# Output projection of a Hymba-style block as seven 2x2-block products of 512 columns, its weight sums made by GpSimd in an earlier stage

## The chip, the cores and the metric

The kernel runs on one core of one Trainium2 chip. Times are device microseconds (us) of one launch. The kernel before took 1847.0 us, the median of three runs (1839.05 to 1862.62 us). A profiled execution of the same kernel took 1841.22 us; all traces below are of that execution, and its span, from the first to the last instruction, is 1839.4 us. PE is TensorE, DVE is VectorE, ACT is ScalarE, POOL is GpSimd, SP is SyncE, which issues nearly all DMAs. PE, DVE, ACT, POOL and SP each run their own instructions in the order in which the program holds them.

## What is computed

One layer on 1024 frames (T) of width 1024, all in float32: a half-step gated feed-forward (SwiGLU), a mixer with one input projection and one output projection, a second half-step feed-forward, and a final norm.

```python
x = x + 0.5 * swiglu(rmsnorm(x, ffn1_norm[l]), ffn1_w_gate[l], ffn1_w_up[l], ffn1_w_down[l])
h = rmsnorm(x, mix_norm[l])
p = h @ w_in[l]
...
x = x + jnp.concatenate([y_a, y_b], axis=-1) @ w_out[l]
x = x + 0.5 * swiglu(rmsnorm(x, ffn2_norm[l]), ffn2_w_gate[l], ffn2_w_up[l], ffn2_w_down[l])
return rmsnorm(x, final_norm)
```

`y_a` (spatial gating) and `y_b` (gated delta rule) are 512 columns each. The change concerns the line with `w_out`: a product of 1024x1024 by 1024x1024.

## The kernel before

Every float32 product is made as three products of a cheaper type: `split` (L60) turns a tile into a high part (a rounding, ACT, L61) and a low part (source less high part, DVE, L62), and `mm3` (L55) adds high x high, high x low and low x high into one PSUM bank. So each new operand costs ACT and DVE one instruction each before PE can use it.

The program runs in five stretches: the gate/up products of the first feed-forward, its down product, the mixer (`middle`), the output projection, and the second feed-forward with its own gate/up and down products. Both feed-forwards are made of 2x2 blocks with seven products in place of eight (the Strassen-Winograd scheme). For their gate/up part the class `Combos` holds the activation's blocks B11, B12, B21, B22 and the sums T1 to T4: `blocks` (L127) transposes a pair of 128-frame tiles with PE, copies and splits the blocks and forms the sums from PSUM on DVE; `put_sums` (L153) splits the sums, with DVE or GpSimd for the low part. `load_gu` (L181) does the same for the weights: GpSimd forms s1 to s4, ACT and DVE split them.

In the down product, `plan` (L359) lists seven products; each is cut into units of two 128-row blocks. `prepare` (L369) loads a unit's two operands, `left` and `right`, over SP, splits them, and runs three units ahead of PE. During products 3 and 4 of this stage GpSimd has next to nothing to do.

The output projection (`w_out`, L571) uses plain blocks. Two groups of four frame tiles, 0,4,1,5 and 2,6,3,7, are transposed and split once (`to_T`, L98). For each group the 1024 output columns are made in four chunks of 256, each of 8 contraction blocks x 4 tiles x 3 products, so the matmuls have 256 columns, and the weights are loaded and split once for each group. The chunk's result is added to the residual tile `xs[t]` by DVE (L593). The first group's tiles are stored, normed in place, transposed and split for the second feed-forward (L609 to L615) after the second group's first two chunks are under way, so the remaining chunks on PE cover that work. Then `start2` makes chunk 0 of the second feed-forward plainly (`gu_plain`): first 256 frames, then the other 256, whose tiles 2, 6, 3, 7 are normed in between. From chunk 1 on PE runs the seven products without pause.

The order on each engine is not written out by hand: a scheduler of the framework arranges the instructions, within what the buffers allow. Buffers come from pools as rings: `graw` has 4 slots (raw weights), `gsp` 7 (split weights), `post` 4, `cmb` 3, PSUM 4 + 4 banks. An allocation waits until the slot's earlier tile has been read for the last time.

Of the kernel before, what the change touches and what calls it, by code (L numbers as in the profile page):

```python
# [30 lines left out]
def block_kernel(ctx: ExitStack, tc, a, out):  # L31
# [75 lines left out]
    class Combos:  # L107
# [19 lines left out]
        def blocks(self, i, pp, xns, uv, b12=None):  # L127
            def tr(j, q):
                return transposed(pp, lambda c: xns[j][:, (q * 4 + c) * P:(q * 4 + c + 1) * P])
# [35 lines left out]
    def ffn(cb, wgu, wd, ps, rp, gp, qp, bp, start, load_xts, emit, before={}, fill=None):  # L165
# [12 lines left out]
        def gtile(dt, name):  # L178
            return gp.tile([P, 2, 512], dt, tag="gsp", name=name, bufs=7)

        def load_gu(c, plain=False):  # L181
            raw = []
            for j in range(2):
                r = rp.tile([P, 1088], F32, tag="graw", name="graw", bufs=4)[:, :D].rearrange("p (s n) -> p s n", s=2)
                nc.sync.dma_start(r, wgu[c][:, j * 1024:(j + 1) * 1024].rearrange("p (s n) -> p s n", s=2))
                raw.append(r)
            a11, a12, a21, a22 = raw[0][:, 0], raw[0][:, 1], raw[1][:, 0], raw[1][:, 1]

            def comb(n, u, v, op):
                f = rp.tile([P, 544], F32, tag="sf", name=n, bufs=4)[:, :512]  # L190
                nc.gpsimd.tensor_tensor(f, u, v, op=op)  # L191
                return f
# [175 lines left out]

        def prepare(l, r, u):  # L369
# [7 lines left out]
            nc.sync.dma_start(left[:, :n], hq[u][:, l, :n])  # L377
# [22 lines left out]
        for k, (_, _, pp, first, last, ev, then) in enumerate(plan):  # L400
# [43 lines left out]
    sp = {n: dr.tile([8, P, 512], F32, tag="sp" + n, name="sp" + n) for n in "zvm"}  # L444
    ba = cp.tile([P, 16, 8], F32, tag="ba", name="ba")[:, :8]
# [13 lines left out]
    with ExitStack() as f1:  # L459
# [83 lines left out]
        ffn(cb, a["f1gu"], a["f1wd"], ps, rp, gp, qp, bp, start1, load_xts, to_mid, {2: [after]}, z0)  # L543
# [14 lines left out]
    with ExitStack() as f2:  # L558
# [10 lines left out]
        xs = load_x(xd, chain(*order))  # L569

        def w_out(i):  # L571
            for ch in range(4):
                ws = []
                for s in range(2):
                    raw = rp.tile([P, 2, 512], F32, tag="graw", name="graw", bufs=4)
                    nc.sync.dma_start(raw, a["wo"][ch][s].rearrange("p (q n) -> p q n", q=2))
                    for q in range(2):
                        w = gp.tile([P, 2, 512], F32R, tag="gsp", name="wo", bufs=7)
                        split(w[:, 0], w[:, 1], raw[:, q])
                        ws.append(w.rearrange("p s (k n) -> p s k n", k=2))  # L580
                yield
                banks = {t: bank(ps[0], "mm")[:, :256] for t in order[i]}
                steps = [(k, t) for k in range(KC // 2) for t in range(4)]
                if (i, ch) == (1, 3):
                    steps.sort(key=lambda s: s[1])
                for q, j in steps:
                    t = order[i][j]
                    for k in (2 * q, 2 * q + 1):
                        w, y = ws[q], yT[i][k // 4][:, :, k % 4, j * P:j * P + P]
                        mm3(banks[t], y[:, 0], y[:, 1], w[:, 0, k % 2], w[:, 1, k % 2], k == 0, k == KC - 1, skip_group_check=True)  # L590
                    if k == KC - 1:
                        xv = xs[t][:, ch * 256:ch * 256 + 256]
                        nc.vector.tensor_tensor(xv, xv, banks[t], op=ALU.add)  # L593
                yield

        cb = Combos(g2, qp, bp)
        pp = (ps[1], "ax")
        together(w_out(0))
        for t in order[0]:
            nc.sync.dma_start(xd[t], xs[t])  # L600

        def b12():
            ts = [gp.tile([P, 2, 512], F32R, tag="gsp", name="B12", bufs=7) for _ in range(2)]
            return [t.rearrange("p s (k n) -> p s k n", k=2) for t in ts]

        second = w_out(1)
        together(second, n=3)
        b = b12()
# [7 lines left out]
        together(second)  # L616
        for t in order[1]:
            nc.sync.dma_start(xd[t], xs[t])

        def start2(f):  # L620
# [11 lines left out]
            V, G = nc.vector, nc.gpsimd  # L632
# [11 lines left out]
        def fin(t, xt):  # L644
            o = gp.tile([P, D], F32, tag="gsp", name="o", bufs=7)
# [17 lines left out]
        ffn(cb, a["f2gu"], a["f2wd"], ps, rp, gp, qp, bp, start2, load_xts, fin, {2: [after]})  # L663
# [14 lines left out]
def middle(tc, nc, a, L):  # L678
# [513 lines left out]
    for h in range(HEADS):  # L1192
# [32 lines left out]
        else:  # L1225
            stage(x, weave(chain(y.values(), y.queries()), islice(u0, 8), (0, 1, 1, 1, 0)), 1.5)
            stage(y, u0, 1)
            u1 = steps("u", 1, ev_u1, part=2)
# [28 lines left out]
def _layout(np, x, ffn1_norm, ffn1_w_gate, ffn1_w_up, ffn1_w_down, mix_norm, w_in, gm_ln_g, gm_ln_b, gm_w_s,  # L1257
# [6 lines left out]
    def tmaj(cols):  # L1264
# [15 lines left out]
        wo=np.stack([tmaj(w_out[0][:, c * 256:c * 256 + 256]) for c in range(4)]),  # L1280
# [26 lines left out]
```

## Time and profile before

| | |
|---|---|
| median of three runs | 1847.0 us |
| the profiled execution | 1841.22 us |
| its span | 1839.4 us |
| mixer's last product ends on PE (about) | 1077.2 us from the span's start |
| output projection ends on PE | 1185.0 us |
| chunk 1 of the second feed-forward starts | 1218.1 us |

The three times in the last rows are read from the timeline of PE. In such a timeline a row gives start, length, engine, line, operation, output, inputs, shapes and count, and in brackets the idle time ahead of it with what ended it. Successive instructions overlap a little, so a row's pace is its length, or the distance to the next start, divided by its count. Where a busy table gives a group's mean duration, that is the latency of one instruction, not its pace.

### The profile page before, as it was taken

To read this page: it belongs to the slowest core of one execution; us is meant where nothing else is said; L and a number is where in the kernel's file an instruction comes from. 1 tells how busy PE (TensorE), PEld (TensorE's weight loads), DVE (VectorE), ACT (ScalarE), POOL (GpSimd) and SP (SyncE) were. 2 spreads that over 40 slices of the span, in tenths; PEclk is the share of its full clock that TensorE was granted. 3 is DMA by queue.
4 is the path that set the end of the run, shared out by engine and by line. 5 is a ranking of instruction groups with operands and counts; after the bars stand their busy time and mean duration, and the time that the engine had idled before them with its cause. 6 is when DMAs were issued, how large, how long until landed. Compare 5 with 4: busy or idle time off the path is not lost.

```text
span 1839.4 us, 25484 instructions
## 1 busy us (share of the span) xinstructions
PE 1784.1 (97%) x9735; PEld 1524.8 (83%) x9735; DVE 1191.7 (65%) x1531; ACT 686.6 (37%) x1193; POOL 747.9 (41%) x583
## 2 busy tenths in 40 slices
PE   5999999999999999898999999999999999999997
PEld 4888888888788889797788989988888888878886
DVE  6867676665565575769655344587776766656546
ACT  6333332333343454432344533452333323243433
POOL 4667666565140012212132420366666665614001
PEclk9999999999999999999999999999999999999999
DMA  5353443544957445453432254334535445495744
GB/s 196 108 175 136 162 152 134 184 158 163 339 188 258 155 177 164 140 195 100 133 94 67 90 197 136 109 104 165 178 132 171 144 154 188 142 344 185 264 142 149
DMA packets 134441, 302.26 MB, mean 164 GB/s; under 512 B 27408, under 2 KB 42032, under 8 KB 134320
## 3 DMA queue, kind: packets, MB, share of 16 engines
q1 hardware_dynamic: 131824, 296.20, 46.9%
q10 hardware_dynamic: 2496, 4.44, 0.8%
q8 instruction: 76, 1.25, 0.3%
q14 instruction: 45, 0.37, 0.1%
HBM read 208.83 MB, written 91.77 MB: 163 GB/s over the span
## 4 chain that ended last, share of the span: by engine, by line
PE 78%; DVE 8%; DMA 5%; POOL 4%; issue 3%; ACT 2%; SPq 0%; POOLq 0%; DVEq 0%; ACTq 0%
PE mm L53 43%; PE ax L53 32%; POOL s L191 1%; POOL t L278 1%; DMA left<-hq 1%; DVE acc L873 1%; PE ax L95 1%; PE sd L53 1%; DMA graw<-in_f1gu_dram 1%; POOL s L278 1%; PE sc L53 1%; DVE T L119 0%; DVE unit L62 0%; DVE wk L62 0%; DVE E L797 0%
## 5 line engine op out<-in xcount | busy, mean ns | idle before, releaser
L53 PE MATMUL mm<-unit 128*128 128x512 f32 x1056 | 244.9, 392 | 4.2 <-ACT unit L61 2.2
L53 PEld LDWEIGHTS mm<-unit 128*128 128x128 f32 x1056 | 198.8, 189 | 47.4 <-ACT unit L61 3.3
L191 POOL TENSOR_TENSOR s<-graw 128x512 f32<-128x512 f32 x84 | 130.3, 1551 | 262.9 <-DMA graw<-in_f2gu_dram 116.0
L62 DVE TENSOR_TENSOR ga<-graw,ga 128x512 fp32r<-128x512 f32 x134 | 155.9, 1166 | 99.9 <-ACT ga L61 99.2
L61 ACT CAST gs<-s 128x512 fp32r<-128x512 f32 x168 | 104.5, 622 | 301.8 <-PE mm L53 151.0
L62 DVE TENSOR_TENSOR unit<-left,unit 128x1024 fp32r<-128x1024 f32 x84 | 101.9, 1215 | 133.0 <-ACT unit L61 132.3
L53 PE MATMUL ax<-T,gs 128*128 128x512 f32 x792 | 183.1, 389 | 0.0
L53 PE MATMUL ax<-unit 128*128 128x512 f32 x792 | 180.5, 389 | 0.0
L53 PEld LDWEIGHTS ax<-T,gs 128*128 128x128 f32 x792 | 148.7, 188 | 30.8
L53 PEld LDWEIGHTS ax<-unit 128*128 128x128 f32 x792 | 148.7, 188 | 30.8
L62 DVE TENSOR_TENSOR gs<-s,gs 128x512 fp32r<-128x512 f32 x168 | 172.7, 1030 | 2.3
L53 PE MATMUL mm<-B,ga 128*128 128x512 f32 (+1 forms) x864 | 166.8, 347 | 3.3 <-ACT B L118 1.9
L61 ACT CAST unit<-left 128x1024 fp32r<-128x1024 f32 x84 | 82.5, 982 | 230.2 <-PE ax L53 100.5
L53 PE MATMUL mm<-T,gs 128*128 128x512 f32 x720 | 166.5, 389 | 0.0
L53 PEld LDWEIGHTS mm<-B,ga 128*128 128x128 f32 x864 | 139.5, 194 | 23.4 <-ACT B L118 2.5
L53 PEld LDWEIGHTS mm<-T,gs 128*128 128x128 f32 x720 | 135.2, 188 | 28.0
L70 POOL TENSOR_TENSOR rs<-rs,half 128x1 f32<-128x1 f32 (+1 forms) x29 | 19.2, 662 | 334.5 <-DVE rs L76 334.4
L53 PE MATMUL mm<-actT,wk 128*128 128x512 f32 x576 | 150.4, 403 | 0.0
L53 PE MATMUL ax<-B,ga 128*128 128x512 f32 x528 | 127.2, 390 | 1.4 <-DVE ga L62 1.4
L53 PE MATMUL mm<-wk,actT 128*128 128x256 f32 x960 | 123.5, 285 | 2.7 <-DVE wk L62 2.7
L53 PEld LDWEIGHTS mm<-wk,actT 128*128 128x128 f32 x960 | 117.4, 190 | 3.4 <-DVE wk L62 3.0
L53 PEld LDWEIGHTS mm<-actT,wk 128*128 128x128 f32 x576 | 103.6, 188 | 18.8
(239 smaller groups left out, 3046.0 us busy)
## 6 DMA issues: line engine op xcount, KB each, us to landing
left<-hq SPq DMA_DIRECT2D x70, 512.0 KB, 5.0
graw<-in_f1gu_dram SPq DMA_DIRECT2D x44, 512.0 KB, 5.4
wq<-t SPq DMA_DIRECT2D x44, 512.0 KB, 2.8
hq<-s SPq DMA_DIRECT2D x44, 512.0 KB, 3.1
graw<-in_f2gu_dram SPq DMA_DIRECT2D x44, 512.0 KB, 4.7
right<-wq SPq DMA_DIRECT2D x40, 512.0 KB, 4.8
wd<-in_f1wd_dram SPq DMA_DIRECT2D x22, 512.0 KB, 6.6
hq<-sg SPq DMA_DIRECT2D x22, 512.0 KB, 3.7
```

The source lines that it names most:

```text
L53: nc.tensor.matmul(*args, **kw)
L61: nc.scalar.copy(h, src)
L62: nc.vector.tensor_tensor(l, src, h, op=ALU.subtract)
L70: nc.gpsimd.tensor_tensor(o, i, half[:, :w], op=ALU.pow)
L95: nc.tensor.transpose(ps[:, i * P:(i + 1) * P], blk(i), ident)
L191: nc.gpsimd.tensor_tensor(f, u, v, op=op)
L278: nc.gpsimd.tensor_tensor(o, u, v, op=op)
L873: nc.vector.scalar_tensor_tensor(acc, pad[:, j:j + 512], cw[:, blk, j:j + 1], acc, op0=ALU.mult, op1=ALU.add)
```

## The change

The output projection takes the 2x2 scheme of the feed-forwards. Frames are halved (tiles 0 to 3 and 4 to 7), the contraction is halved (`y_a`, `y_b`), and the output columns are halved. Seven products of 512 frames x 512 x 512 are made: each has 4 tiles x 4 contraction blocks x 3 = 48 matmuls with 512 columns, 336 in all, where there were 768 with 256 columns. The activation goes through `Combos.blocks` and `put_sums` (T1 and T3 with GpSimd's low part), so it needs the four sums and their splits beside the blocks. The sums of the weights s1 to s4 are formed by GpSimd during products 3 and 4 of the first feed-forward's down stage (`wo_sums`, stepped by `side`), stored to DRAM in `wos`, and loaded as raw weights later. Each weight is loaded and split once. The results are combined by DVE (from PSUM) and GpSimd (into the residual tiles).

The last two products, B22 and T4, are made for frame tiles 0 and 1 first, and then for 2 and 3; the norm, transposes and splits of the pairs 0,4 and 1,5 for the second feed-forward stand between. Their block B12 now lies in two of the four `graw` slots. The ring of split weights has 8 slots in the second feed-forward, and the mixer's last product takes its tiles in the order 0,4,1,5,2,6,3,7. The weights `wo` come in plain rows.

```diff
+        def wo_sums():
+            for k in range(4):
+                raw = []
+                for j in range(2):
+                    raw.append(rp.tile([P, 1088], F32, tag="graw", name="graw", bufs=4)[:, :D])
+                    nc.sync.dma_start(raw[j], a["wo"][4 * j + k])
+                (a11, a21), (a12, a22) = ((r[:, :512], r[:, 512:]) for r in raw)
+                s1, s2, s3, s4 = s = [rp.tile([P, 544], F32, tag="sf", name="ws", bufs=4)[:, :512] for _ in range(4)]
+                for o, u, v, op in ((s1, a21, a22, ALU.add), (s2, s1, a11, ALU.subtract), (s3, a11, a21, ALU.subtract), (s4, a12, s2, ALU.subtract)):
+                    nc.gpsimd.tensor_tensor(o, u, v, op=op)
+                yield
+                yield
+                for i in range(4):
+                    nc.sync.dma_start(wos[k][:, i], s[i])
+                yield
...
+                if k in (3, 4):
+                    with tc.issue_after(queued[-1].ins):
+                        next(side, None)
...
-        order = ((0, 4, 1, 5), (2, 6, 3, 7))
-        yT = acts()
-        for i in range(2):
-            for j, t in enumerate(order[i]):
-                to_T((ps[1], "ax"), lambda c: yblk(t, c), j, yT[i])
...
+        steps = (("B11", (0, 0)), ("B21", (0, 1)), ("T2", 1), ("T1", 0), ("T3", 2), ("B22", 3), ("T4", (1, 1)))
+
+        def weights(n):
+            r, ws = steps[n][1], []
+            for j in range(2):
+                raw = rp.tile([P, 2, 512], F32, tag="graw", name="graw", bufs=4)
+                if isinstance(r, tuple):
+                    w = a["wo"][4 * r[1] + 2 * j:4 * r[1] + 2 * j + 2][:, :, r[0] * 512:r[0] * 512 + 512]
+                else:
+                    w = wos[2 * j:2 * j + 2][:, :, r]
+                nc.sync.dma_start(raw, w.rearrange("k p n -> p k n"))
+                for k in range(2):
+                    w = gp.tile([P, 2, 512], F32R, tag="gsp", name="wo", bufs=8)
+                    split(w[:, 0], w[:, 1], raw[:, k])
+                    ws.append(w)
+            return ws
+
+        def product(n, ws, banks, tiles, first, last, ev):
+            y = cy.B[steps[n][0]]
+            for t in tiles:
+                sl = slice(t * P, t * P + P)
+                for k in range(4):
+                    mm3(banks[t], y[:, 0, k, sl], y[:, 1, k, sl], ws[k][:, 0], ws[k][:, 1], first and k == 0, last and k == 3, skip_group_check=True)
+                ev(t, banks[t])
...
+        ws = [weights(0), weights(1)]
+        for i in range(4):
+            uv = cy.sums()
+            together(cy.blocks(i, X, lambda j, c: yblk(i + 4 * j, c), uv))
+            together(cy.put_sums(i, ("T2", "T1", "T3", "T4"), (V, G, G, V)))
...
+        product(0, ws[0], ba_, range(4), True, False, lambda t, p: nc.scalar.copy(p1[t], p))
+        ws.append(weights(2))
+        xs.update(load_x(xd, order))
...
+        def last(tiles):
+            product(5, ws[5], ba_, tiles, False, True, ev_a)
+            product(6, ws[6], bx, tiles, False, True, ev_x)
+
+        last((0, 1))
+        b = [rp.tile([P, 2, 512], F32R, tag="graw", name="B12", bufs=4).rearrange("p s (k n) -> p s k n", k=2) for _ in range(2)]
+        pp = X
         for i in range(2):
             xi = xs[i], xs[i + 4]
             uv = cb.sums()
...
             together(cb.blocks(i, pp, xi, uv, b))
             together(cb.put_sums(i, ("T1", "T3"), (nc.gpsimd, nc.gpsimd)))
-        together(second)
...
+        last((2, 3))
```

What stands where on the engines, at the places that the prediction speaks of. First DVE at the head of the output projection. Before, its first rows are the low parts of the transposed tiles (`actT`, from PSUM bank `ax`), then those of the weights (`wo`); a tile's number tells one from the next:

```order
L103 TENSOR_TENSOR actT_9471<-ax_9549,actT_9471 128x4x128
L103 TENSOR_TENSOR actT_9470<-ax_9556,actT_9470 128x4x128
L103 TENSOR_TENSOR actT_9471<-ax_9563,actT_9471 128x4x128
L103 TENSOR_TENSOR actT_9470<-ax_9570,actT_9470 128x4x128
L103 TENSOR_TENSOR actT_9471<-ax_9577,actT_9471 128x4x128
L62 TENSOR_TENSOR wo_9602<-graw_9600,wo_9602 128x512
L62 TENSOR_TENSOR wo_9605<-graw_9600,wo_9605 128x512
```

Sixteen `actT` rows stood there, and 4 rows of weights were enough for the first chunk. Now DVE has these rows for the third pair of tiles and the beginning of the fourth; `f` holds the sums, B11_9533 is the block that the first product uses, ax_9697 is the bank of the fourth pair:

```order
L119 TENSOR_TENSOR T4_9536<-f_9614,T4_9536 128x4x128
L119 TENSOR_TENSOR B11_9533<-ax_9656,B11_9533 128x4x128
L119 TENSOR_TENSOR B21_9590<-ax_9670,B21_9590 128x4x128
L150 TENSOR_TENSOR f_9655<-ax_9677,f_9654 128x512
L139 TENSOR_TENSOR f_9695<-ax_9705,f_9695 128x512
L152 TENSOR_TENSOR f_9655<-ax_9670,f_9655 128x512
L119 TENSOR_TENSOR B22_9535<-ax_9677,B22_9535 128x4x128
L119 TENSOR_TENSOR T2_9534<-f_9655,T2_9534 128x4x128
L119 TENSOR_TENSOR T4_9536<-f_9655,T4_9536 128x4x128
L119 TENSOR_TENSOR B11_9533<-ax_9697,B11_9533 128x4x128
```

The last of these is the 34th row of DVE since the mixer; of the 34, eight are splits of weights, six are splits of T2 and T4, and 20 read a PSUM bank.

Next GpSimd where the second feed-forward begins. `rs` are the four powers that the norms of tiles 2, 6, 3, 7 wait for, `s1` to `s4` the weight sums of chunk 1. Before:

```order
L191 TENSOR_TENSOR s1_11055<-graw_11050 128x512
L191 TENSOR_TENSOR s2_11057<-s1_11055,graw_11048 128x512
L191 TENSOR_TENSOR s3_11065<-graw_11048,graw_11050 128x512
L191 TENSOR_TENSOR s4_11073<-graw_11048,s2_11057 128x512
L70 TENSOR_TENSOR rs_10713<-rs_10713,half_70 128x1
L70 TENSOR_TENSOR rs_10719<-rs_10719,half_70 128x1
L70 TENSOR_TENSOR rs_10727<-rs_10727,half_70 128x1
L119 TENSOR_TENSOR T4_11029<-f_10223,T4_11029 128x4x128
L70 TENSOR_TENSOR rs_10733<-rs_10733,half_70 128x1
```

and now:

```order
L70 TENSOR_TENSOR rs_10389<-rs_10389,half_70 128x1
L70 TENSOR_TENSOR rs_10395<-rs_10395,half_70 128x1
L70 TENSOR_TENSOR rs_10403<-rs_10403,half_70 128x1
L119 TENSOR_TENSOR T4_10705<-f_10191,T4_10705 128x4x128
L119 TENSOR_TENSOR T4_10705<-f_10249,T4_10705 128x4x128
L193 TENSOR_TENSOR s1_10731<-graw_10726 128x512
L70 TENSOR_TENSOR rs_10409<-rs_10409,half_70 128x1
L193 TENSOR_TENSOR s2_10733<-s1_10731,graw_10724 128x512
```

All four powers stood behind chunk 1's sums; now three stand ahead of them, and the fourth, rs_10409, behind s1, which reads the raw weights graw_10726 of chunk 1.

Last the queue of SP at the same place. `xd` are stores of residual tiles, the first two `graw` are chunk 0's raw weights, the next two chunk 1's. Before:

```order
L576 DMA graw_10565<-in_wo_dram 128x1024
L185 DMA graw_10693<-in_f2gu_dram 128x1024
L185 DMA graw_10695<-in_f2gu_dram 128x1024
L185 DMA graw_11048<-in_f2gu_dram 128x1024
L185 DMA graw_11050<-in_f2gu_dram 128x1024
L618 DMA xd_72<-x_9592 128x1024
```

and now:

```order
L632 DMA xd_72<-x_9826 128x512
L187 DMA graw_10369<-in_f2gu_dram 128x1024
L187 DMA graw_10371<-in_f2gu_dram 128x1024
L632 DMA xd_72<-x_9830 128x512
L632 DMA xd_72<-x_9824 128x512
L632 DMA xd_72<-x_9828 128x512
L187 DMA graw_10724<-in_f2gu_dram 128x1024
L187 DMA graw_10726<-in_f2gu_dram 128x1024
```

The raw weights of both chunks stood ahead of the last group's stores; now chunk 0's stand behind the store of tile 6 (x_9826) and chunk 1's behind the last store of all.

More of the change, by code (lines that the diff above doesn't have):

```diff
@@ L163, in together, with ffn @@
             pass
-    def ffn(cb, wgu, wd, ps, rp, gp, qp, bp, start, load_xts, emit, before={}, fill=None):
+    def ffn(cb, wgu, wd, ps, rp, gp, qp, bp, start, load_xts, emit, before={}, fill=None, side=iter(()), wide=64, ng=7):
         A, X = (ps[0], "mm"), (ps[1], "ax")
@@ L596, in block_kernel @@
[L596 to L608, printed above, removed]
+        order = 0, 4, 1, 5, 2, 6, 3, 7
+        cy, cb = Combos(None, qp, bp), Combos(g2, qp, bp)
@@ new lines, in block_kernel, with ev @@
+        p1, e = ([b[t // 2][:, t % 2] for t in range(4)] for b in (pt, et))
+        ba_, bx = ([bank(*p) for _ in range(4)] for p in (A, X))
+        product(0, ws[0], ba_, range(4), True, False, lambda t, p: nc.scalar.copy(p1[t], p))
+        ws.append(weights(2))
+        xs.update(load_x(xd, order))
+        def ev(t, p):
+            add(V, xh(t, 0), p)
+            store(t, 0)
+        product(1, ws[1], ba_, range(4), False, True, ev)
+        ws.append(weights(3))
+        def ev(t, p):
+            add(V, p1[t], p)
+            add(G, xh(t, 1), p1[t])
+            add(G, xh(t + 4, 0), p1[t])
@@ new lines, in block_kernel, with ev @@
+        product(2, ws[2], bx, range(4), True, True, ev)
+        ws.append(weights(4))
+        ba_ = [bank(*A) for _ in range(4)]
+        def ev(t, p):
+            V.tensor_tensor(e[t], p, p1[t], op=ALU.add)
+            add(G, xh(t + 4, 1), e[t])
+        product(3, ws[3], ba_, range(4), True, False, ev)
+        ws.append(weights(5))
+        bx = [bank(*X) for _ in range(4)]
+        def ev(t, p):
+            add(V, xh(t + 4, 1), p)
+            store(t + 4, 1)
+        product(4, ws[4], bx, range(4), True, False, ev)
```

73 lines of the change are left out of this document (36 added, 37 removed).

## The prediction

> **What bounds the kernel now.** I read the page's busy table and its chain first, then the timeline of PE around the output projection, then DVE, ACT and GpSimd there.
>
> ```profile
> span 1839.4 us, 25484 instructions
> PE 1784.1 (97%) x9735; PEld 1524.8 (83%) x9735; DVE 1191.7 (65%) x1531; ACT 686.6 (37%) x1193; POOL 747.9 (41%) x583
> PE 78%; DVE 8%; DMA 5%; POOL 4%; issue 3%; ACT 2%; SPq 0%; POOLq 0%; DVEq 0%; ACTq 0%
> ```
>
> PE is the bound, so less PE work is worth its time wherever PE stays fed. The next two groups of rows are the timeline of PE from the mixer's end to chunk 1, and one row of the chain for the pace of 512 columns.
>
> ```profile
> 1077.18 0.60 PE L95 MATMUL ax<-ident,ya 128*128 128x128 f32 x4
> 1077.61 0.60 PE L95 MATMUL ax<-ident,oh 128*128 128x128 f32 x4
> ...
> 1089.49 57.38 PE L53 MATMUL mm<-wo,actT 128*128 128x256 f32 x476 [2.52 <-DVE wo L62]
> ...
> 1185.04 1.84 PE L53 MATMUL mm<-B,ga 128*128 128x256 f32 x14
> ...
> 1197.88 1.91 PE L95 MATMUL ax<-ident,xn 128*128 128x128 f32 x16
> ...
> 1206.08 12.18 PE L53 MATMUL mm<-B,ga 128*128 128x256 f32 x94
> 1218.10 2.91 PE L53 MATMUL ax<-B,ga 128*128 128x512 f32 x12
> ```
> ```profile
> 81.56 19.04 PE mm L53 x84
> ```
>
> From 1077.18 to 1218.10 the output projection and the start of the second feed-forward fill 140.9 us, nearly without gaps. A 256-column matmul goes at 57.38 / 476 = 0.1205 us, a 512-column one at 19.04 / 84 = 0.2267 us, and four transposes at 0.43 us.
>
> **What is removed on PE.** 768 x 0.1205 = 92.6 us of matmuls go, 336 x 0.2267 = 76.2 us come: 16.4 us less. The 64 transposes of the mixer's output stay. Everything now hangs on how much of the 16.4 us is given back as waiting. TensorE: Matmul & The Clock Gate of the Trainium skill (Back-to-back issue gap) says that a warm matmul costs its columns at 2.4 GHz plus some 2.5 ns; by that the saving would be 768 x 109.2 less 336 x 215.8 ns = 11.4 us, 5 us smaller. The rows of this trace are slower in both sizes (120.5 and 226.7 ns) and carry 14 ns of fixed cost in each, so the rows decide.
>
> **The head.** Before the seven products, ACT, DVE and GpSimd must make sums that were not needed so far. DVE at the head, in the same place and elsewhere:
>
> ```profile
> 1078.43 4.35 DVE L103 TENSOR_TENSOR actT<-ax,actT 128x512 fp32r<-128x512 f32 x7 [20.59 <-ACT actT L102]
> ...
> 1088.76 4.89 DVE L62 TENSOR_TENSOR wo<-graw,wo 128x512 fp32r<-128x512 f32 x8
> ...
> 1209.63 3.78 DVE L119 TENSOR_TENSOR T<-f,T 128x512 fp32r<-128x512 f32 x4
> 1213.33 5.18 DVE L62 TENSOR_TENSOR gs<-s,gs 128x512 fp32r<-128x512 f32 x3
> ```
> ```profile
> 1149.83 1.29 POOL L119 TENSOR_TENSOR T<-f,T 128x512 fp32r<-128x512 f32 x1 [5.61 <-ACT T L118]
> 1175.91 1.29 POOL L191 TENSOR_TENSOR s<-graw 128x512 f32<-128x512 f32 x1 [15.93 <-DMA graw<-in_f2gu_dram]
> 1181.03 0.55 POOL L70 TENSOR_TENSOR rs<-rs,half 128x1 f32<-128x1 f32 x1
> ```
>
> A DVE operation that reads PSUM takes 4.35 / 7 = 0.62 us. One with both inputs in SBUF takes 4.89 / 8 = 0.61 us where GpSimd rests, 3.78 / 4 = 0.94 us where it is partly busy, and 5.18 / 3 = 1.73 us where it never stops. The first product reaches frame tile 3 only when B11 of the fourth pair is split, the 34th DVE operation of the head: 20 from PSUM and 14 within SBUF. GpSimd has nine sums and splits of 1.29 us in the same time, so it is partly busy and I take 0.94: 20 x 0.62 + 14 x 0.94 = 25.6 us from 1078.43, that is 1104.0. ACT is faster (about 30 casts, 2.65 us for five in the row below) and so no bound. Then come the first product's last tile (12 x 0.2267 = 2.7 us) and the whole second product (48 x 0.2267 = 10.9 us): 1117.6. With 0.61 for the 14 it would be 1112.9, with 1.73 1128.6. PE's own work would end at 1077.18 + 6.9 (transposes) + 21.8 = 1105.9, so some 12 us of PE wait are made here.
>
> **The middle.** T2, T1 and T3 follow, 10.9 us each, and the first half of B22 and T4, 10.9 us. In each 10.9 us DVE has four weight splits and at most eight 0.62 us evacuations (8.7 us even at 0.94), GpSimd twelve additions in 33 us, about 16 us at 1.29. Both hide behind PE, and so does the reading of `wos`; bounded at 0 to 2 us if one split is late. End of that half, E = 1117.6 + 43.5 = 1161.1.
>
> **The tail.** Here cover is lost. Before, the first pairs' norm, transposes and splits ran beside a good 32 us of output projection. Now only the second half of the last two products (10.9 us) is left beside them.
>
> ```profile
> 1135.47 0.41 DVE L593 TENSOR_TENSOR x<-x,mm 128x256 f32<-128x256 f32 x1
> ...
> 1156.43 0.68 DVE L119 TENSOR_TENSOR B<-ax,B 128x512 fp32r<-128x512 f32 x1
> ...
> 1188.91 1.28 DVE L82 SCALAR_TENSOR_TENSOR xn<-x,rs,grow 128x1024 f32<-128x1024 f32 x1 [0.66 <-POOL rs L70]
> ...
> 1194.69 2.31 DVE L82 SCALAR_TENSOR_TENSOR xn<-x,rs,grow 128x1024 f32<-128x1024 f32 x1 [1.69 <-POOL rs L70]
> ```
> ```profile
> 1194.62 1.29 POOL L119 TENSOR_TENSOR T<-f,T 128x512 fp32r<-128x512 f32 x1
> ```
> ```profile
> 1077.81 2.65 ACT L102 CAST actT<-ax 128x512 fp32r<-128x512 f32 x5
> ...
> 1197.03 0.34 ACTq L66 DMA_DIRECT2D grow<-in_final_norm_dram  x1
> 1197.47 1.28 ACT L243 ACT_TABLE_LOAD   x1 [4.73 <-DVE xn L82]
> ...
> 1199.31 0.59 ACT L133 COPY f<-ax 128x512 f32<-128x512 f32 x1
> ```
> ```profile
> graw<-in_f2gu_dram SPq DMA_DIRECT2D x44, 512.0 KB, 4.7
> wd<-in_f2wd_dram SPq DMA_DIRECT2D x22, 512.0 KB, 6.8
> left<-hq SPq DMA_DIRECT2D x70, 512.0 KB, 5.0
> right<-wq SPq DMA_DIRECT2D x40, 512.0 KB, 4.8
> ```
>
> From the last addition into those tiles (1135.9) to the last split of their blocks (1157.0) 21.1 us passed. The same chain starts at E, one 0.7 us addition later; its other additions are wider (+0.5), and a split of chunk 0's second weight, at 0.94, follows: PE has what it needs for most of the first `gu_plain` at E + 23.2. But PE's own work ends at E + 14.4, so it waits about 6 us, less what it can do with partial operands. Then a chain over a buffer: the raw weights of chunk 1 take the slots of B12, and SP can load them only when PE has read B12, 20 matmuls later (E + 25.6). They land after 4.7 us (E + 30.3); GpSimd makes s1 (1.29) and only then the fourth power (0.55); DVE norms the last tile. That norm took 1.28 us alone, and 2.31 where it began 0.07 us after a GpSimd operation of 1.29; the next operation on GpSimd, s2, would do the same here, so I take 2.3: E + 34.5. What is queued behind that s1 on GpSimd is the power; behind the norm on ACT is the load of the next gain, and behind it the copies of the next blocks. Before, from that norm's end at 1197.0 to the restart of PE at 1206.08 took 9.1 us; the table load and activations that lay in it (1197.47 to 1199.31) now lie ahead of the gain's load, which leaves 7.2: E + 41.7. Then 12.0 us of products as before (1206.08 to 1218.10), so chunk 1 starts at E + 53.7 = 1214.8, against 1218.1. **The sum is 3.3 us less.** PE's own work from E to chunk 1 is 10.9 + 192 x 0.1205 + 64 transposes, 41.0 us, so this tail can at most be 12.7 us shorter; a 6.8 us landing makes it 2.1 longer.
>
> **The sums in the first down stage.** The windows of products 2 to 5 there:
>
> ```profile
> 557.00:586.90 29.90, 29.90 (x134) 24.77 (x133) 15.38 (x17) 11.15 (x12) 0.00 (x0) 1.00 0.72 254
> 586.90:616.90 30.00, 30.00 (x134) 24.85 (x133) 18.18 (x21) 13.47 (x17) 0.00 (x0) 1.00 0.70 225
> 616.90:646.80 29.90, 29.90 (x133) 24.78 (x132) 15.38 (x17) 11.85 (x13) 0.00 (x0) 1.00 0.33 109
> ```
> ```profile
> 562.50 1.05 ACT L61 CAST unit<-left 128x1024 fp32r<-128x1024 f32 x1 [3.44 <-PE ax L53]
> ...
> 563.58 1.23 DVE L62 TENSOR_TENSOR unit<-left,unit 128x1024 fp32r<-128x1024 f32 x1 [1.46 <-ACT unit L61]
> 564.72 1.22 DVE L62 TENSOR_TENSOR unit<-right,unit 128x1024 fp32r<-128x1024 f32 x1
> ```
>
> The columns after the window are its length and the busy time of PE, PEld, DVE, ACT and POOL, then clock, DMA share and GB/s. GpSimd's 16 sums at 1.29 us (1.73 at worst) are 21 to 28 us in 60 where it does nothing, and DVE has 12 us free in each 30. On SP come 8 loads and 16 stores, 8.4 MB: 140 GB/s on top of 240, which would be near full, but the third window moves 109, so the prefetch can give way. Behind a store that waits for GpSimd stand `left` and `right` loads; a unit's split starts when a buffer comes free two units (10.9 us) ahead of its use and takes 1.05 + 2 x 1.22 = 3.5 us, and a store stands two units behind its loads, which is about as long as landing plus sums (5.0 + 5.2). I take 0; with that cover gone, one late `right` costs its landing, 4.8 us. The changed tile order in the mixer costs nothing, since PE is dense there.
>
> **The rivals.** (1) DVE and GpSimd do not disturb each other and PE stays nearly fed: the head at 1112.9 and a tail a few us shorter, 4.7 + 5 us better, a gain of 13 us. For it: the 0.61 us row; against it: nine GpSimd operations stand in that very stretch. (2) Slower: GpSimd's operations stop DVE's splits at the head. If each of the nine holds up DVE for its 1.29 us, 34 x 0.61 + 11.6 = 32.4 us, and the head ends 6.8 us later, at 1124.4, a loss of 3.5 us in all; at the 1.73 us pace it ends at 1128.6, a loss of 7.7 us. It decides from 3.3 us up, that is when the 14 splits average over 0.94 + 3.3 / 14 = 1.18 us. For it speak the `gs` row and the norm of 2.31 us, against it that GpSimd pauses between blocks. SBUF — State Buffer of the Trainium skill (Who interferes with whom) says that a DVE instruction with two SBUF inputs and a GpSimd instruction that reads SBUF exclude each other for a whole instruction; the norm that lasted about its own time plus the rest of GpSimd's operation agrees with it. (3) The sums do not hide: SP is held in the first down stage, one to three late units, 4.8 to 14 us, a net loss of 1.5 to 11 us. Against it: POOL 0.00 and the units' lead. (4) The change does not do what it says: PE's saving is waited away entirely, 0 us; that is the border of (2).
>
> **How the numbers follow.** The profiled execution took 1841.2 us, and the sum gives 1837.9. The median of the runs shown stands 5.8 us above that execution; a new median should lie between, so I add half, 2.9 us: 1841. Forecast (gain of 0 to 8 us): 0.5. Rival 1, 1841.2 - 13 + 2.9, around 1831: 0.18. Rival 2 with 4, 1844 to 1852: 0.22. Rival 3, 1845 to 1855: 0.06. Beyond these: 0.04. The range from 1827 (rival 1 with hardly any offset) to 1853 (rivals 2 and 3) holds 8 in 10. A 2% change is 37 us, about what a measurement of this kernel can tell from no change; no term here reaches it, for PE's whole saving is 16.4 and the largest loss bounded here is 11. So 0.96 for the same, 0.02 for each side.
>
> **What would show it.** In the changed profile: 336 matmuls with 512 columns at 0.227 us; the second product ending near 1117 us; the 14 splits at 0.9 us each; 10.9 us products without gaps after that; PE idle some 6 us in the first `gu_plain`, put down to DVE's splits; chunk 1's raw load issued only after B12's last matmul, and s1 ahead of the last power; chunk 1 near 1215; no PE idle at 557 to 650. The prediction is wrong if the head ends before 1110 or after 1124, if PE idles in the first down stage, or if anything after chunk 1 changes pace.

## The result and the profile after

The changed kernel took 1858.28 us, the median of 20 runs, against 1847.63 us for the kernel before in 20 runs beside it. The ratio is 1.0054, with a 95% interval of 1.0038 to 1.0071: about 10 us slower. The forecast was 1841 us, from a sum that gave a gain of 3.3 us; the result lies above its range (1827 to 1853 us). The profiled execution took 1858.39 us, 17.2 us more than the one of before, which was a short one of its kernel (1841.22 us against the median of 1847.63).

First the page's opening rows:

```profile
span 1856.6 us, 24769 instructions
PE 1775.2 (96%) x9303; PEld 1497.2 (81%) x9303; DVE 1205.8 (65%) x1535; ACT 693.8 (37%) x1209; POOL 794.3 (43%) x623
```

PE is busy for 8.9 us less than before and the span is 17.2 us longer, so PE waits 26 us more. Nearly half of that is in one place. These are the windows of products 4 and 5 of the first down stage, cut as the prediction showed them (window, length, busy time of PE, PEld, DVE, ACT and POOL, clock, DMA share, GB/s):

```profile
586.90:616.90 30.00, 29.12 (x128) 23.57 (x127) 19.37 (x15) 10.31 (x11) 13.72 (x8) 1.00 0.83 309
616.90:646.80 29.90, 18.45 (x73) 14.43 (x72) 15.54 (x18) 11.98 (x14) 0.00 (x0) 0.77 0.76 260
```

Before, both windows were full on PE, at a clock of 1.00. Now 11.45 us of the second are idle, and the granted clock is 0.77. The timeline of PE shows the hole and what it is put down to. First product 5 before, in one run without a wait, then the changed kernel:

```profile
616.70 30.08 PE L53 MATMUL ax<-unit 128*128 128x512 f32 x132
```
```profile
599.77 19.88 PE L53 MATMUL mm<-unit 128*128 128x512 f32 x87
630.45 0.80 PE L53 MATMUL ax<-unit 128*128 128x512 f32 x1 [10.80 <-ACT unit L61]
631.90 31.56 PE L53 MATMUL ax<-unit 128*128 128x512 f32 x131 [0.65 <-DVE unit L62]
663.30 3.33 PE L53 MATMUL mm<-unit 128*128 128x512 f32 x14
```

Product 5 now starts at 630.45 and not at 616.70, and it lasts 32.85 us and not 29.92. Product 6 starts 16.7 us late. The chain is followed back from PE's wait to ACT, from ACT to a DMA, and from that to SP. ACT's timeline at that place, before (one row) and after:

```profile
605.61 1.20 ACT L61 CAST wz<-zraw 128x544 fp32r<-128x544 f32 x2 [1.18 <-DMA zraw<-in_wz_dram]
```
```profile
611.60 0.63 ACT L61 CAST unit<-right 128x512 fp32r<-128x512 f32 x1 [2.89 <-DMA right<-wq]
627.31 1.19 ACT L61 CAST wz<-zraw 128x544 fp32r<-128x544 f32 x2 [15.09 <-DMA zraw<-in_wz_dram]
628.41 1.04 ACT L61 CAST unit<-left 128x1024 fp32r<-128x1024 f32 x1
629.36 1.04 ACT L61 CAST unit<-right 128x1024 fp32r<-128x1024 f32 x1
```

ACT has nothing to do for 15 us, because the next instruction in its order is the cast of `zraw`, the raw weights of the mixer's first product, which PE uses only after the whole down stage (from 698.62 on). Behind it stand the casts of product 5's first unit, for which PE waits. The operands of that unit were there in time: its `right` was issued at 613.98 and landed 4.3 us later, at 618.3, before PE ran out of work at 619.65. On SP, the same stretch of the kernel before and after:

```profile
601.33 0.33 SPq L525 DMA_DIRECT2D zraw<-in_wz_dram  x1
```
```profile
559.45 6.06 SPq L565 DMA_DIRECT2D wos<-ws  x4
...
576.00 4.98 SPq L565 DMA_DIRECT2D wos<-ws  x4
...
593.82 6.17 SPq L565 DMA_DIRECT2D wos<-ws  x4
...
600.52 0.44 SPq L557 DMA_DIRECT2D graw<-in_wo_dram  x1
...
610.62 3.27 SPq L565 DMA_DIRECT2D wos<-ws  x3
...
618.68 0.46 SPq L533 DMA_DIRECT2D zraw<-in_wz_dram  x1
```

A DMA that waits for nothing occupies SP for 0.32 us or so, four of them for 1.3. The four stores of one group of sums take up to 6.17 us, since SP stands at them until GpSimd has made the sums. Ahead of the first of the four SP stands too, and these rows do not count that time: SP comes to the first store at 553.4, and the row begins at 559.45, when GpSimd has finished the first sum. The table of SP's waits holds all of it (total, times, longest):

```profile
SPq L565 <- POOL ws L561: 39.0, 16, 6.5
```

Over the four groups SP stood 39.0 us at stores. GpSimd in turn waits for the group's raw weights, and those are loaded by the same SP, behind the stores of the group ahead:

```profile
573.92 2.06 POOL L561 TENSOR_TENSOR ws<-graw 128x512 f32<-128x512 f32 x1 [8.76 <-DMA graw<-in_wo_dram]
...
592.50 1.30 POOL L561 TENSOR_TENSOR ws<-graw 128x512 f32<-128x512 f32 x1 [11.85 <-DMA graw<-in_wo_dram]
```

So the groups form a closed ring: store, load, landing, sums, store. From the first group's stores to the fourth's, 559.45 to 610.62, a turn takes 17.1 us. PE uses up the three units that belong to a group in 15.0 us. With every turn SP falls further behind, and at the end `zraw` is issued 17.35 us later than before. It also takes longer to land, 8.6 us where it took 4.3 to 5.0 before: the loads that were held back go out together, and the first window below shows the DMA engines at a share of 1.03.

What the wait costs beyond its own length is seen in windows of 5 us:

```profile
622.00:627.00 5.00, 0.00 (x0) 0.00 (x0) 0.00 (x0) 0.00 (x0) 0.00 (x0) 0.50 1.03 411
627.00:632.00 5.00, 0.90 (x2) 0.39 (x2) 3.88 (x5) 4.69 (x7) 0.00 (x0) 0.50 0.61 217
632.00:637.00 5.00, 5.00 (x15) 3.99 (x16) 5.00 (x7) 3.28 (x4) 0.00 (x0) 0.67 0.91 309
637.00:642.00 5.00, 5.00 (x24) 4.13 (x23) 4.93 (x6) 2.01 (x2) 0.00 (x0) 1.00 0.44 121
```

The granted clock falls to 0.50 while PE waits and stays low for about 5 us after the restart: 15 matmuls in a window that holds 24 at full clock. That makes product 5 some 2.3 us longer on top of its second wait (0.65 us).

The output projection itself went nearly as forecast. The timeline of PE from the mixer's end to chunk 1:

```profile
1097.76 1.03 PE L95 MATMUL ax<-ident,ya 128*128 128x128 f32 x8
...
1137.78 11.04 PE L53 MATMUL ax<-wo,T 128*128 128x512 f32 x48
...
1175.86 5.60 PE L53 MATMUL ax<-wo,T 128*128 128x512 f32 x24
...
1203.29 7.94 PE L53 MATMUL mm<-B,ga 128*128 128x256 f32 x64 [0.30 <-DVE ga L62]
...
1219.64 1.08 PE L95 MATMUL ax<-ident,xn 128*128 128x128 f32 x4 [6.67 <-DVE B L119]
...
1225.00 11.88 PE L53 MATMUL mm<-B,ga 128*128 128x256 f32 x94
1236.71 2.91 PE L53 MATMUL ax<-B,ga 128*128 128x512 f32 x12
```

From 1097.76 to 1236.71 are 138.95 us, where it was 140.92: 2.0 us less.

### The profile page after: what moved, and what is told of

The parts are those of the page before. It is cut to its first block, busy times and chain, and to the rows that moved or that the text cites. A ratio compares the mean times of both kernels' runs of the same rounds, so it can differ in the third digit from the quotient of the medians.

```text
span 1856.6 us, 24769 instructions
## 1 busy us (share of the span) xinstructions
PE 1775.2 (96%) x9303; PEld 1497.2 (81%) x9303; DVE 1205.8 (65%) x1535; ACT 693.8 (37%) x1209; POOL 794.3 (43%) x623
## 5 line engine op out<-in xcount | busy, mean ns | idle before, releaser
L62 DVE TENSOR_TENSOR gs<-s,gs 128x512 fp32r<-128x512 f32 x168 | 176.7, 1054 | 48.8 <-ACT gs L61 47.0
L53 PE MATMUL ax<-unit 128*128 128x512 f32 x792 | 182.8, 392 | 11.5 <-ACT unit L61 10.8
L193 POOL TENSOR_TENSOR s<-graw 128x512 f32<-128x512 f32 x84 | 124.3, 1480 | 144.7 <-DMA graw<-in_f1gu_dram 84.7
L53 PEld LDWEIGHTS ax<-unit 128*128 128x128 f32 x792 | 149.9, 189 | 43.5 <-ACT unit L61 11.2
L62 DVE TENSOR_TENSOR unit<-left,unit 128x1024 fp32r<-128x1024 f32 x84 | 105.9, 1262 | 119.9 <-ACT unit L61 119.7
L62 DVE TENSOR_TENSOR ga<-graw,ga 128x512 fp32r<-128x512 f32 x134 | 146.0, 1092 | 53.7 <-ACT ga L61 52.7
L61 ACT CAST ga<-graw 128x512 fp32r<-128x512 f32 x134 | 83.0, 622 | 130.8 <-PE mm L53 46.0
L62 DVE TENSOR_TENSOR unit<-right,unit 128x1024 fp32r<-128x1024 f32 x84 | 109.9, 1308 | 28.0 <-ACT unit L61 27.9
```

The source lines that it names most:

```text
L53: nc.tensor.matmul(*args, **kw)
L61: nc.scalar.copy(h, src)
L62: nc.vector.tensor_tensor(l, src, h, op=ALU.subtract)
```

## The experiments

After the first two profiles there were three theories. A: the loss is made in the first down stage, because SP stands at stores that wait for GpSimd; it reaches PE by the late `zraw` and by ACT's order (A1), or simply by late unit loads (A2). B: the new output projection loses. C: the sums load the DMA engines or GpSimd too much, whoever issues them.

**The sums alone.** The kernel before, with `wo_sums` in products 3 and 4; `wos` is stored and read by nobody. (The weights lie in another layout there, so the sums have other values; their sizes and number are the same.)

```diff
-        ffn(cb, a["f1gu"], ..., {2: [after]}, z0)
+        ffn(cb, a["f1gu"], ..., {2: [after]}, z0, wo_sums())
```

> The kernel before, with the sums of the output weights formed, stored and read by nobody, in products 3 and 4 of the first down stage. Theory A (the loss is made there: SP's queue stands behind stores that wait for GpSimd, so loads go out late): 9 to 16 us slower than before, ratio 1.005 to 1.009, with PE idle 8 to 12 us as product 5 of that stage begins. Theory B (the output projection itself is the loss, the sums hide): ratio 0.999 to 1.001 and no PE idle in the down stage.

It took 1863.22 us, a ratio of 1.0093 (1.006 to 1.0125): 17 us slower with the old projection. The hole stands at the same place in its timeline of PE:

```profile
631.13 0.79 PE L53 MATMUL ax<-unit 128*128 128x512 f32 x1 [9.18 <-ACT unit L61]
```

**The projection alone.** The changed kernel without `wo_sums`; the four products with sums take plain halves of `wo` in their place.

```diff
-                    w = wos[2 * j:2 * j + 2][:, :, r]
+                    w = a["wo"][2 * j:2 * j + 2][:, :, r % 2 * 512:r % 2 * 512 + 512]
```

> The changed kernel without the sums: nothing is formed or stored in the down stage, and where the products need sums of weights they load plain halves of the weights in their place (so four of seven products use other weights). Theory A: 2 to 5 us faster than before, ratio 0.997 to 0.999, chunk 1 of the second feed-forward at 1214 to 1217 us, the down stage without PE idle. Theory B: as slow as the changed kernel, ratio 1.004 to 1.006.

It took 1841.06 us, 0.9965 (0.9941 to 0.9988) of the kernel before, with no PE wait in products 3 to 5. The two runs split the change: the projection gains 2 to 11 us, the sums cost 0.9% or 16.4 us (1.0054 less 0.9965). B falls.

**The same sums, stores issued by GpSimd.** Loads, sums, bytes and places are those of the changed kernel; only the queue of the 16 stores differs.

```diff
-                    nc.sync.dma_start(wos[k][:, i], s[i])
+                    nc.gpsimd.dma_start(wos[k][:, i], s[i])
```

> The changed kernel with the 16 stores of the sums issued by GpSimd, behind its own sums, and no longer by SP. Theory A: nothing on SP waits for GpSimd, PE idles under 2 us at the start of product 5, ratio to before 0.997 to 1.000. Theory C (the transfers themselves are too many in that stage, or GpSimd slows DVE's splits): PE idles as in the changed kernel, ratio 1.004 to 1.006.

It took 1841.91 us, 0.997 (0.9945 to 0.9995): by the ratios 15.5 us (1.0054 less 0.997) are gone by one line, and the kernel is faster than both. SP no longer waits at any of these stores. Each issue takes GpSimd 0.54 us, where it took SP 0.32. Its windows of products 3 and 4:

```profile
557.00:587.00 30.00, 30.00 (x134) 24.86 (x133) 20.56 (x18) 11.17 (x12) 20.17 (x18) 1.00 1.03 401
587.00:617.00 30.00, 30.00 (x134) 24.82 (x134) 20.71 (x23) 13.45 (x16) 10.45 (x13) 1.00 0.90 320
```

The traffic is heavier than in the changed kernel (401 GB/s at a share of 1.03 in the first window, where it was 255), and PE waits for nothing. C falls for this place. A store on GpSimd's own queue comes when GpSimd has made the sums, so it holds up nothing there but the next group. DMA: Bandwidth & Descriptors of the Trainium skill (Rules for kernel authors) says that spreading DMAs over SP, ACT and GpSimd does not help bandwidth and saves only issue time. For bandwidth nothing here speaks against it; but the queue that a waiting DMA stands in decided 15.5 us.

**The fill of the mixer's weights one product later.** The stores stay on SP; `zraw` and its casts come in product 6.

```diff
-            if k == 5 and fill is not None:
+            if k == 6 and fill is not None:
```

> The changed kernel with the z weights (their two loads and four casts on ACT) begun one product later, at product 6 in place of 5. Theory A1 (the late load reaches PE through ACT: the casts of z weights wait for it, with the casts of product 5's units behind them): PE idle at product 5 falls from 10.8 to under 3 us, ratio to before 0.998 to 1.001. Theory A2 (the units' own left and right loads are late): PE idles 8 us or more, ratio 1.004 to 1.006.

It took 1843.79 us, 0.9987 (0.9962 to 1.0012). SP is held nearly as long as in the changed kernel (37.9 us of waiting at the stores), but the late load that stood first in ACT's order is gone:

```profile
591.14 6.17 SPq L565 DMA_DIRECT2D wos<-ws  x4
```
```profile
618.05 30.00 PE L53 MATMUL ax<-unit 128*128 128x512 f32 x131 [0.76 <-DVE unit L62]
```

So at this place the way is A1: the unit loads behind the stores come nearly in time by themselves (0.76 us of wait), and the cast of `zraw` makes the rest.

**The sums beside products 0 and 1.** There SP has no `zraw` to load, so A1 alone would expect hardly any loss.

```diff
-                if k in (3, 4):
+                if k in (0, 1):
```

> Changed kernel, with the sums formed beside products 0 and 1 of the first down stage in place of 3 and 4; the same 8 loads and 16 stores on SP. In products 0 and 1 SP has no zraw load to issue and ACT no cast of the mixer's first weights. Theory A (the stores that wait on SP for GpSimd do their harm by way of the late zraw loads and ACT's casts of them, which stand ahead of the unit casts): PE idles at most 3 us in 497 to 650 and the ratio to the kernel before is 0.996 to 1.000, as with the fill one product later (0.9987). Rival A2 (a store that holds SP does the same harm wherever it stands, since left and right loads queue behind it): 8 to 17 us of PE idle and slow clock, moved to 510 to 570; ratio 1.002 or more.

It took 1860.55 us, 1.0074 (1.0047 to 1.0102), as the rival A2 expected. Its window of product 2, and the wait of ACT in it:

```profile
527.00:557.00 30.00, 20.87 (x69) 15.41 (x68) 21.84 (x15) 12.79 (x16) 23.05 (x13) 0.77 0.82 303
```
```profile
529.98 0.62 ACT L61 CAST unit<-right 128x512 fp32r<-128x512 f32 x1 [13.44 <-DMA right<-wq]
```

Here a unit load itself is late: it was issued at 521.93, and stood on SP behind eight loads of `x` (9.51 us) and four stores (4.16 us). Which load suffers, and whether PE feels it, depends on what stands behind the stores.

**The same place, stores by GpSimd.** Both edits above together.

> Sums formed beside products 0 and 1 of the first down stage, with their stores issued by GpSimd in place of SP: the earlier run at that place (ratio 1.0074, clock 0.77 and 20.87 us of PE work in 527 to 557) with the holding of SP alone taken away. Theory (stores that wait at the head of SP's queue for GpSimd keep back the unit loads behind them, at either place): at most 2 us of PE idle in 497 to 560, clock near 1.00, ratio 0.996 to 0.999. Rival (at this place the traffic of the sums beside the eight loads of x, or GpSimd's sums ahead of its own additions of x, make the loss): 6 us or more of PE idle there remain and the ratio stays at 1.004 or above.

1853.14 us, 1.0021 (0.9998 to 1.0044). The window shows neither theory whole:

```profile
527.00:557.00 30.00, 27.25 (x111) 21.63 (x110) 22.20 (x16) 13.23 (x16) 27.04 (x18) 0.94 0.92 335
```

PE still idles 2.75 us here and 2.83 us in the 30 us ahead, where it was 9.13 and 1.96 with the stores on SP. Of the ratio's excess over the best placing (0.997), half goes with the stores' queue. The rest comes from what else is at that place. Candidates are the loads of `x`, GpSimd's own additions, and the stores of `hq`, which stand on SP and wait for GpSimd as well (9.3 us of waiting in 470 to 650, where it was 4.8 before); they were not separated.

**The stores three units behind their loads.** The prediction had taken two units as enough. The stores stay on SP.

```diff
-                if k in (3, 4):
+                if (2, 5) <= (k, u) <= (4, 5):
...
                 yield
                 yield
+                yield
                 for i in range(4):
                     nc.sync.dma_start(wos[k][:, i], s[i])
-                yield
```

> Changed kernel with the stores left on SP in the place of products 3 and 4, but each group of stores three units behind its loads in place of two (the first loads one unit sooner, with the last unit of product 2). It tests the step of the prediction that two units are about as long as landing plus sums. In the changed kernel each of the four groups held SP for 3 to 6 us. Theory (the distance is one unit, 5 us, too short): a group holds SP for under 2 us, PE idles at most 2 us in 557 to 650, ratio 0.997 to 0.9995. Rival (SP runs so far ahead that the stores reach its head early at any distance, since a unit loads as soon as a buffer comes free): holds of 3 us and more remain and PE idles 5 us or more around 620; ratio above 1.002.

1850.08 us, 0.9994 (0.9973 to 1.0015). The time is the theory's; the holds and PE's wait lie between theory and rival:

```profile
551.51 5.45 SPq L566 DMA_DIRECT2D wos<-ws  x4
...
566.96 5.18 SPq L566 DMA_DIRECT2D wos<-ws  x4
...
584.61 6.17 SPq L566 DMA_DIRECT2D wos<-ws  x4
...
598.15 3.94 SPq L566 DMA_DIRECT2D wos<-ws  x3
...
607.27 0.75 SPq L533 DMA_DIRECT2D zraw<-in_wz_dram  x1
```

The rows of the stores are about as long as in the changed kernel, so SP still reaches them early. But it stands there for less time in all:

```profile
SPq L566 <- POOL ws L561: 28.6, 15, 5.1
```

That is 28.6 us where it was 39.0. The ring now turns in 15.5 us (551.51 to 598.15 in three turns) and starts 8 us sooner, so `zraw` is issued at 607.27 and not at 618.68, and PE waits 3.03 us for ACT and 0.65 behind it. For PE it counts when the last hold ends, against the time at which the loads behind it are needed.

**The head of the projection.** On top of the stores by GpSimd, the second product's weights are split behind the four pairs' blocks, so that DVE reaches the block that the first product needs last with three splits fewer.

```diff
-        ws = [weights(0), weights(1)]
+        ws = [weights(0)]
         for i in range(4):
...
+        ws.append(weights(1))
```

> Changed kernel with the stores of the sums issued by GpSimd, and the four weight splits of the second product moved behind the blocks of all four pairs, so that B11 of the fourth pair is the 31st DVE operation of the head and not the 34th. It tests the term of the sum for the head (20 reads of PSUM at 0.62 and 14 splits at 0.94 us bound it; measured so far 40.2 us from the mixer's last product to T2). Theory (DVE's chain is the bound): three splits fewer at 0.94 to 1.05 us are 2.8 to 3.2 us, of which the second product may give back some, so the head is 37 to 39.5 us and the ratio to the kernel before 0.995 to 0.997 (0.997 with the stores alone). Rival (PE waits there for ACT, for banks or for the first product's weights): head 40 to 41 us, ratio unchanged.

1840.08 us, 0.998 (0.9958 to 1.0003). The head did not get shorter: PE resumes with the last tile at 1104.20 in the row below, 26.3 us after the mixer's last product (1077.86 in its timeline), where it was 26.7, and T2's run of matmuls, one of them done ahead, starts 40.8 us after that product, where it was 40.0.

```profile
1104.20 4.16 PE L53 MATMUL mm<-wo,B 128*128 128x512 f32 x17 [1.51 <-DVE B L119]
```

The three splits saved 0.4 us. They were cheap ones: in the changed kernel the second product's four splits took 2.56 us, 0.64 each, while GpSimd stood idle (1105.56 to 1112.85). The one of them that still stands ahead now takes 1.66 us, beside a GpSimd operation, so the 11 splits left take 12.17 us where 14 took 13.07, and DVE waits 1.25 us for ACT's casts and PE's transposes (0.85 in the changed kernel). So the mean of 0.94 us is no price for taking one split out. What else bounds the head, the four PSUM banks or GpSimd, is open.

**The tail.** On top of the stores by GpSimd, `s1` of chunk 1 is placed behind the fourth power on GpSimd.

```diff
+            with tc.issue_after(lastp.pop().ins) if lastp else nullcontext():
+                s1 = comb("s1", a21, a22, ALU.add)
```

> Changed kernel with the stores of the sums issued by GpSimd, and s1 of chunk 1 put behind the fourth power on GpSimd. It tests the step of the tail in which the last norm waits for s1, and s1 for raw weights that wait for B12's slots. With it ahead the power started at 1214.25, its input was ready at 1211.55. Theory (that order costs the tail): the power starts within 1 us of its input, the wait of PE ahead of the last transposes falls from 6.67 to 4 to 5 us, and chunk 1 starts 1.7 to 2.7 us sooner after E (55.4 us in the changed kernel); ratio to the kernel before 0.9955 to 0.9965. Rival (another chain ends as late: the norms of the tiles ahead of it, or GpSimd's T splits): the wait stays above 6 us and the ratio at 0.997.

1839.11 us, 0.9972 (0.995 to 0.9994). The power now starts 1.0 us after its input is ready (1191.52), where it was 2.7, but the wait of PE falls by only 0.86 us:

```profile
1198.76 1.08 PE L97 MATMUL ax<-ident,xn 128*128 128x128 f32 x4 [5.81 <-DVE B L121]
```

GpSimd comes to the power only after two T splits, at 1192.56, and the norm of the last tile takes 2.27 us there as it took 2.28 in the changed kernel. Chunk 1 starts at E + 55.6 (E is the end of the first half of the last two products, as in the prediction), no sooner than the changed kernel's 55.4: the 94 matmuls ahead of it took 13.31 us and not 11.88, and the granted clock in 1200 to 1210 was 0.50 and 0.69. Against the stores by GpSimd alone (0.997) no difference can be told.

**All three edits together.**

> All three edits together: stores of the sums issued by GpSimd, the second product's weight splits behind the blocks, s1 behind the fourth power. If head and tail add, ratio to the kernel before 0.994 to 0.9955, some 1836 to 1839 us against 1847; if neither edit matters, 0.997, as with the stores alone.

1843.34 us, 0.9993 (0.9965 to 1.0022), runs from 1836.82 to 1858.32. Neither edit adds anything that these runs can tell. In the profiled execution the wait at the tail is 5.80 us, as above, and chunk 1 starts at E + 53.8, with 11.97 us for the 94 matmuls. So in these two executions what the edit of the tail gave back went with how long the clock stayed low behind the wait. Of the complete kernels the stores by GpSimd, with or without the edit of the tail, are the ones whose whole interval lies below the kernel before.

## Why the prediction was wrong

**The step that failed** is the term for the sums in the first down stage: "a store stands two units behind its loads, which is about as long as landing plus sums (5.0 + 5.2). I take 0". It was put at 0 and measured about 16 us (the sums alone 1.0093; the changed kernel with and without them 1.0054 and 0.9965), and SP stood 39.0 us at the stores. Three things in it were wrong:

- The sizes. The raw weights landed in 6.9 us (median of the eight loads, which took 5.2 to 9.4) and not 5.0, and the four sums took 6.7 to 7.7 us, since some of them last up to 2.3 us and not 1.29. Landing plus sums is about 14 us, and two units are about 10.
- The pricing by one late load. Loads of a group stand behind the stores of the group ahead on the same queue. That closes a ring with a turn of 17.1 us against 15.0 us of PE's work, so lateness adds up over four turns.
- The list of what is queued behind. The prediction named `left` and `right`. It left out `zraw`, which stands there too, and whose casts stand ahead of product 5's unit casts on ACT. Moving the fill alone removed nearly all of PE's wait.

The rival for this case was there ("SP is held in the first down stage, one to three late units, 4.8 to 14 us", a net loss up to 11 us). Its net loss was near the truth (about 10 us), though the term itself, 16 us, lay beyond its 14. It got 6 in 100 for a wrong reason: that POOL stood at 0.00 and that the units have a lead. An idle GpSimd says that its work finds room; it says nothing of a queue of another engine that must wait for that work.

**What held.** The head was put at 40.4 us, from the mixer's last product to the end of the second product; it took 40.0 (1097.76 to 1137.78). The 14 splits within SBUF were put at 0.94 us each; they took 0.93 (13.07 us in all). That the mean came out is in part luck: it was taken from another place, and single splits took 0.64 to 1.5 us. That their number sets the head is not borne out: three fewer saved 0.4 us. The middle was put at 43.5 us and took 43.5 (to 1181.30), without a wait. The changed tile order of the mixer cost nothing: its last product fills 22.7 us in both.

**The tail was mis-sized by 1.7 us.** From E, now 1181.30, chunk 1 was put at E + 53.7 and came at E + 55.4. The gate of the first `gu_plain` came at E + 22.0 and not 23.2, and PE waited 0.30 us at it, not the 6 us that were to show there; it had made a third of that part's matmuls ahead of the gate. The power behind `s1` started at 1214.25, E + 33.0, 1.4 us later than worked out. The chain over B12's slots, which the prediction made the bound, was not what `s1` waited for: the raw weights had landed by 1211.7, and GpSimd was still in two T splits until 1212.6, which stand ahead of `s1` in its order and which the sum left out. `s1` then took 1.71 us in place of 1.29. The norm behind it took 2.28 us as foreseen, beside `s2` and `s3` on GpSimd (1214.76 to 1218.19), and from its end to the restart it was 7.9 us where 7.2 were taken. That the norm lasts longer there agrees with SBUF — State Buffer of the Trainium skill (Who interferes with whom), by which a DVE instruction with two SBUF inputs contends with a GpSimd instruction that reads SBUF.

**The sum for the projection** was a gain of 3.3 us; between the two profiles it is 2.0 us, and with the sums left out the kernel is 5.6 us faster by the medians, in an interval of 2.2 to 10.9 us. The rest of the 17.2 us between the two profiles is the mixer, 3.9 us longer there. From the transposes at its beginning to its end it took 427.4 us in the profile of before and 431.3 after; in the experiments' executions it was 429.4 to 444.0, with the old mixer order and only the sums added 430.7. So the profile of before caught a short one, and no step of the change is shown to make the difference. Behind the start of chunk 1 both profiles take about the same, 621.3 us before and 619.9 after.

## What to carry to other kernels

Before a step with a store is put into a stage with a full prefetch queue, write down the queue that issues it, row by row, past the stage's end: everything behind a DMA that must wait for a computation waits too, and it then delays whatever stands behind its own consumer on the next in-order engine. Where the loads of a step share the queue with the stores of the step ahead, work out the turn of that ring and hold it against the time that the covering work takes for one turn. Above it lateness adds up (17.1 us against 15.0 here); in the run with the stores by GpSimd a turn took 13.5 us (552.01 to 592.60 in three turns of its sums), and PE waited for nothing. Stores of computed data belong on the queue of the engine that computes them, or behind every load that is needed soon; beside products 0 and 1 that took away half of the loss, not all.

## What the runs showed of the hardware

- After a wait of 10.8 us the granted clock was 0.50, and about 5 us passed from the restart before it was 1.00 again. A wait of 6.67 us at the tail did the same (windows of 5 us at 0.55 and 0.50), and so did one of 3.03 us (the stores three units behind; clock 0.89 over 617 to 647), so a wait of PE can cost more than its length, 2.3 us in the first case. In windows of 0.5 us the clock falls 2.0 us after the last matmul has ended (619.65) in the first case, and 2.0 us after (616.71) in the third.
- TensorE: Matmul & The Clock Gate of the Trainium skill (What's actually happening) gives half clock after an idle window of some 3.4 us and full clock after as long a busy one. The two levels agree; the times do not quite: here 2.0 us without work were enough, and the return took 4.8 to 6.1 us from the restart.
- The core's DMA engines moved 401 GB/s over 30 us and 411 GB/s over 5 us, at a share of 1.03, and in the first case PE did not wait. DMA: Bandwidth & Descriptors of the Trainium skill (Specifications) puts the limit from HBM at about 358 GB/s for a core and the fabric's at 435. The measured figures lie between the two; part of this traffic is stores, and no run separates reads from writes.
